# Early loads into a larger buffer class, convolution and gate tiles in turn, and the last expert tiles by token half, in a two-block transformer kernel

## The chip, the cores and the metric

The kernel runs as one program on one core of one Trainium2 chip. The metric is the time of one execution on the device in microseconds (us), of which lower is better.

## The reference, cut to what is computed

Two blocks run one after the other on a batch of one with 256 tokens (T) of width 1024 (D), all in float32. The first block is a gated mixer, whose two halves (block attention MoBA and a chunked mLSTM) read projections of one normed and modulated input; the modulation rows come from a product with `ada_w`. The second block adds a memory cross-attention and a PEER expert layer, twice, and a last norm:

```python
mod = jnp.dot(silu(c), ada_w[l]) + ada_b[l]                  # 6 rows of 1024
h = modulate(rms_norm(x, norm1_g[l]), sh1, sc1)
z = jnp.einsum('bsd,de->bse', h, w_in[l]) + b_in[l]
mq, mk, mv, mo, mi, mf, aq, ak, av, ga, gb = split(z)
qk = silu(causal_dwconv(concat([mq, mk]), conv_w[l], conv_b[l]))
ya = moba_attention(rope(aq), rope(ak), av)                  # 8 heads, softmax over 256 keys
ym = rms_norm(mlstm_chunkwise(q, k, mv, mi, mf)) * sigmoid(mo)
merged = sigmoid(ga) * (ym @ p_mlstm[l]) + sigmoid(gb) * (ya @ p_moba[l])
x = x + g1 * (merged @ w_out[l])
...                                                          # gated feed-forward, then block two
for l in range(2):
    h = h + mixer(rmsnorm(h)); h = h + memory_cross_attn(rmsnorm(h), rmsnorm(mem), wq, wkv, wo)
    h = h + peer_ffn(rmsnorm(h), wq, sub_keys, u, v)         # 128 tiles of 128 experts
return rmsnorm(h, final_norm)
```

## The kernel before, in words

**Products.** A weight tile of 128 by 1024 numbers is loaded as part of a 1 MB transfer (`raw`, two tiles each), issued on SP's queue by `stream()` (L358). `split()` makes of each tile a rounded copy `wH` on ACT (L335) and the rest `wL` on DVE (L336). TensorE (PE) then makes three products for each 128x128 piece: L400 (`nH`, `wH`), L401 (`nL`, `wH`) and L402 (`nH`, `wL`), where `nH` and `nL` are the same two parts of the input. `lin_t` gives an output tile with 24 such matmuls of 256 columns from one weight tile (8 pieces). `lin_n` (L430 to L432) gives the natural layout with 512 columns, 12 matmuls for a weight tile. The pool `wraw` has 3 `raw` buffers; `wspl` has 3 of `wH` and 3 of `wL`. Everything with pool `None` lies in size classes: the largest, `c2064`, has 12 buffers.

**First block, in order.** `mem_kv(0)` makes the keys of the memory from `wk0`, unsplit, in one pass of f32 matmuls (L398), and the values from `wv0` (`lin_n`). While the generator `kv` steps through 12 steps, the loop in `first_block` puts other work between them: `ada` steps, each of which loads 1 MB of `ada_w` and makes two rows with two DVE instructions (`adaj`, L598, 128x1024); `rope_tables` at step `RI` = 5 (some fifteen DVE instructions, then cosine and sine on ACT); and from step 4 on one `n1.chunk` a step. A chunk squares a part of x on ACT (L219) and adds it on POOL, and the eighth on DVE (L223). `n1.sums` sums over the partitions on PE (L203); `n1.bc` takes the power on POOL (L473, `pow_col`), and PE (L460) and DVE (L465) spread it as `rbc`.

Then `w_in` is multiplied. Its 37 transposed tiles come in the order in which `w_in_t` is packed: the mLSTM gates, 8 rotary tiles (RoPE), 8 convolution tiles, 4 output gates (`smo`), 16 merge gates (`sg`). `evac` takes a tile out of PSUM. A convolution tile costs ACT three instructions and DVE four (`conv`, L699 three times and L702); a gate tile costs ACT one. The natural tiles `w_in_n` are four weight pairs: two before, and two later in `rest()`, after 8 of the tiles that follow. From the ninth tile on, these products are the *filler* of `moba` (L955 scores, `sme` softmax on DVE and ACT in L483 to L491, L500 transposes, L512 to L514 values) and `mlstm`. Every third filler step adds an `ada` step (`AS` = 3); what is left of the 12 later `ada` steps runs in `w_out` (`AW` = 3).

**PEER and end.** In `v_tile`, 128 expert tiles are accumulated into four PSUM banks `y` (token half `tb` by output half `hf`), 12 matmuls of 512 columns each (L1500), first all of token half 0, then of 1. After layer 0, four copies (`py`, L1525), transposes (L1531) and adds to x (L1533) follow. After layer 1, `final` adds y to x (L1625), squares (L1627), takes the power, multiplies by r and the norm's row in one DVE instruction (L1633), and writes out.

The order on each engine is made by a scheduler from the program; each engine then runs its own list in that order.

Of the kernel before, what the change touches and what calls it, by code (L numbers as in the profile page):

```python
# [17 lines left out]
ALU = mybir.AluOpType  # L18
# [12 lines left out]
VL, RI, MD, UX, M1, M2, D1, D2, AS, AW, PQ0, NQ0, FT, F0, FH, FS, FL, FO = 6, 5, 1, 4, 1.25, 1.5, 0.5, 0.75, 3, 3, 13, 3, 0.6, 1, 0.5, 1, 4, 1.075  # L31
# [63 lines left out]
def layout(i):  # L95
# [13 lines left out]
    A["w_in_t"] = _pack_t(np.concatenate([gate, w_in[:, 2056:3080], w_in[:, 0:1024], w_in[:, 1536:2048], w_in[:, 3592:5640]], axis=1))  # L109
# [174 lines left out]
class Prog:  # L284
# [73 lines left out]
    def stream(self, name, head=None, split=True, order=None):  # L358
        ap = self.A[name]
        n = ap.shape[0]  # L360
        for i in [2 * j for j in order] if order else range(0, n, 2):
            k = min(2, n - i)
            if head is None or i:
                raw = self.t(self.wraw, "raw", [P, 2, 1024])
                self.nc.sync.dma_start(raw[:, :k], ap[i:i + k].rearrange("n p f -> p n f"))
            else:
                raw = head
# [202 lines left out]
    def mem_kv(self, l, nm, head=None):  # L570
# [12 lines left out]
        if head is None:  # L583
            yield from self.lin_t(f"wk{l}", 8, 8, nm.hs, evac, norm=nm)
        else:
            yield from self.lin_t(f"wk{l}", 8, 8, None, evac, st=self.stream(f"wk{l}", head, False), norm=nm, whole=self.memg)
# [66 lines left out]
    def first_block(self):  # L653
# [16 lines left out]
        for i in range(12):  # L670
            next(kv)
            if i % 3:
                next(ada)
            if i == 1:
                nc.sync.dma_start(self.x, A["xT"])
            if i == RI:
                cos, sin = self.rope_tables()
            if 4 <= i:
                n1.chunk(i - 4)
        n1.sums()  # L680
        n1.bc
# [32 lines left out]
        def evac(e, ps):  # L714
# [9 lines left out]
            elif e < 17:  # L724
                raw = self.t(None, "qraw", [P, T])
                nc.scalar.activation(raw, ps, AF.Identity, bias=self.vec("b_qk", e - 9))  # L726
                conv(e - 9, raw)
            elif e < 21:
                nc.scalar.activation(smo[:, e - 17], ps, AF.Tanh, scale=0.5, bias=hb[:, e - 17:e - 16])
            else:  # L730
                nc.scalar.activation(sg[:, e - 21], ps, AF.Tanh, scale=0.5, bias=hb[:, e - 17:e - 16])
# [20 lines left out]
        def rest():  # L752
            for _ in range(8):
# [34 lines left out]

        for g in (self.lin_t("p_moba", 8, 4, (ya[:, :4], ya[:, 4:]), ev_ma), self.lin_t("p_mlstm", 8, 4, (ym[:, :4], ym[:, 4:]), ev_mm)):
            self.run(g)  # L790
# [5 lines left out]
        for i, _ in enumerate(self.lin_t("w_out", 8, 8, (mH, mL), self.residual(n2, lambda e: self.mod[:, 16 + e:17 + e]))):  # L796
            if i % AW == AW - 1:
# [567 lines left out]
    def peer(self, l, nm):  # L1365
# [117 lines left out]

        def v_tile(n):
# [11 lines left out]
            for tb in range(2):  # L1496
                sl = slice(tb * P, tb * P + P)
                for a, m in ((wh, vH), (wh, vL), (wl, vH)):
                    for hf in range(2):
                        nc.tensor.matmul(y[tb * 2 + hf], a[:, sl], m[:, hf * 512:hf * 512 + 512], start=n == 0 and a is wh and m is vH, stop=n == P - 1 and a is wl)  # L1500
# [21 lines left out]
        for g in range(2):  # L1522
            for tb in range(2):
                yt = self.t(None, "py", [P, 512])
                (nc.scalar.copy if tb else nc.vector.tensor_copy)(yt, y[tb * 2 + g])  # L1525
                ys.append(yt)
        for g in range(2):
            for tb in range(2):
                ps = self.sm()
                for c in range(4):  # L1530
                    nc.tensor.transpose(ps[:, c * P:c * P + P], ys[g * 2 + tb][:, c * P:c * P + P], self.ident)  # L1531
# [86 lines left out]
    def final(self, y, xn, frow):  # L1618

        nc = self.nc  # L1620
        for tb in range(2):
            ss = self.t(None, "fss", [P, 2])
            for hf in range(2):
# [3 lines left out]
                nc.scalar.activation(junk, xs, AF.Square, accum_out=ss[:, hf:hf + 1])  # L1627
            nc.vector.tensor_add(ss[:, :1], ss[:, :1], ss[:, 1:])
            r = self.pow_col(ss[:, :1], 1.0 / D, EPS, 1)
            for hf in range(2):  # L1630
                sl = slice(hf * 512, hf * 512 + 512)
                o = self.t(None, "fo", [P, 512])
                nc.vector.scalar_tensor_tensor(out=o, in0=xn[:, tb, sl], scalar=r, in1=frow[:, sl], op0=ALU.mult, op1=ALU.mult)  # L1633
# [29 lines left out]
```

## Time and profile before

| | us |
|---|---|
| median of 3 runs (lowest to highest) | 2528.02 (2525.88 to 2528.76) |
| the profiled execution's own time | 2529.0 |
| its span in the trace | 2527.3 |
| PE busy | 2481.3 (98%) |
| DVE busy | 1887.2 (75%) |
| ACT busy | 1293.1 (51%) |
| POOL busy | 94.5 (4%) |

The span is what the trace covers; the time holds 1.7 us more. Busy times are of the engine's own instructions, and PE's contain matmuls that overlap. In the chain of waits that ended last, PE has 82% of the span and DVE 8%; in the groups by line, the expert products L1500 are the largest, and the line with most idle time of PE ahead of it is L398 (the memory's keys).

### The profile page before, as it was taken

Reading aid. Unit: us, or ns where it says so; the run is one execution under the profiler, and the core shown is the slowest. Engines: PE = TensorE matmul, PEld = TensorE weight load, DVE = VectorE, ACT = ScalarE, POOL = GpSimd, SP = SyncE. Lnnn points to the kernel's source line nnn. Section 1 sums busy time; section 2 is a strip of 40 time slices with the busy share of each in tenths; the row PEclk is TensorE's granted clock in tenths of the full one; section 3 lists DMA queues with packets and bytes.
Section 4 is the critical chain, followed back from the end, with each engine's and each line's share of the span. In section 5 each row is a group of like instructions: output and inputs, shape, how many; then the busy total and the mean of one; then the engine's idle time right before and its main releaser. Section 6 shows DMA issues by size and latency. Waiting matters only on the chain.

```text
span 2527.3 us, 44009 instructions
## 1 busy us (share of the span) xinstructions
PE 2481.3 (98%) x17668; PEld 2297.1 (91%) x17668; DVE 1887.2 (75%) x3438; ACT 1293.1 (51%) x2102; POOL 94.5 (4%) x107
## 2 busy tenths in 40 slices
PE   8999999999999999999999999999999999999998
PEld 6879999999999999999888889899999989998887
DVE  7887876686898976555777798767999755556776
ACT  3554555455455555444444563645455544444544
POOL 1000100221000000000000100110000000000000
PEclk9999999999999999999999999999999999999999
DMA  8556565554555796567875544345457866579753
GB/s 336 183 181 229 204 230 205 184 169 150 173 175 199 273 313 221 194 222 241 296 257 193 191 172 150 117 150 167 168 192 270 312 221 212 202 241 298 277 187 130
DMA packets 197468, 536.20 MB, mean 212 GB/s; under 512 B 9232, under 2 KB 82192, under 8 KB 191760
## 3 DMA queue, kind: packets, MB, share of 16 engines
q1 hardware_dynamic: 197264, 533.40, 61.2%
q8 instruction: 138, 2.26, 0.4%
q14 instruction: 66, 0.54, 0.1%
HBM read 492.47 MB, written 40.89 MB: 211 GB/s over the span
## 4 chain that ended last, share of the span: by engine, by line
PE 82%; DVE 8%; issue 6%; DMA 2%; ACT 1%; POOL 0%; SPq 0%; DVEq 0%; POOLq 0%; ACTq 0%
PE mm L1500 23%; PE mm L400 9%; PE mm L401 9%; PE mm L402 9%; PE sm L400 8%; PE sm L401 8%; PE sm L402 8%; DVE wL L336 2%; PE sm L1462 1%; PE sm L1463 1%; PE mm L431 1%; PE mm L432 1%; PE mm L430 1%; DMA gt<-gate_dram 1%; DMA raw<-in_wk 1%
## 5 line engine op out<-in xcount | busy, mean ns | idle before, releaser
L335 ACT CAST wH<-raw 128x1024 fp32r<-128x1024 f32 x789 | 826.6, 1049 | 992.4 <-PE sm L401 312.9
L336 DVE TENSOR_TENSOR wL<-raw,wH 128x1024 fp32r<-128x1024 f32 x789 | 966.8, 1226 | 455.4 <-ACT wH L335 449.8
L400 PE MATMUL sm<-uH,wH 128*128 128x256 f32 x2048 | 584.3, 285 | 2.1 <-ACT wH L335 2.0
L402 PE MATMUL sm<-uH,wL 128*128 128x256 f32 x2048 | 577.3, 282 | 3.8 <-DVE wL L336 3.8
L401 PE MATMUL sm<-uL,wH 128*128 128x256 f32 x2048 | 578.6, 283 | 0.0
L400 PE MATMUL mm<-nH,wH 128*128 128x256 f32 (+1 forms) x1432 | 410.6, 288 | 4.6 <-ACT qraw L726 2.4
L401 PE MATMUL mm<-nL,wH 128*128 128x256 f32 (+1 forms) x1432 | 404.8, 283 | 1.2 <-DVE nL L616 1.0
L402 PE MATMUL mm<-nH,wL 128*128 128x256 f32 (+1 forms) x1432 | 403.6, 283 | 0.8 <-DVE wL L336 0.6
L400 PEld LDWEIGHTS sm<-uH,wH 128*128 128x128 f32 x2048 | 386.3, 189 | 6.6 <-ACT wH L335 2.5
L402 PEld LDWEIGHTS sm<-uH,wL 128*128 128x128 f32 x2048 | 386.0, 189 | 5.6 <-DVE wL L336 5.6
L401 PEld LDWEIGHTS sm<-uL,wH 128*128 128x128 f32 x2048 | 386.7, 189 | 3.6
L1500 PE MATMUL mm<-wH,pwh 128*128 128x512 f32 x1024 | 317.6, 391 | 4.0 <-ACT pwh L335 4.0
L1500 PE MATMUL mm<-wL,pwh 128*128 128x512 f32 x1024 | 316.8, 391 | 0.0
L1500 PE MATMUL mm<-wH,pwl 128*128 128x512 f32 x1024 | 316.3, 390 | 0.0
L400 PEld LDWEIGHTS mm<-nH,wH 128*128 128x128 f32 x1432 | 270.1, 189 | 9.8 <-issue 3.5
L401 PEld LDWEIGHTS mm<-nL,wH 128*128 128x128 f32 x1432 | 270.9, 189 | 2.1 <-DVE nL L616 1.2
L402 PEld LDWEIGHTS mm<-nH,wL 128*128 128x128 f32 x1432 | 270.2, 189 | 2.5 <-DVE wL L336 1.4
L1500 PEld LDWEIGHTS mm<-wL,pwh 128*128 128x128 f32 x1024 | 192.8, 188 | 41.2
L1500 PEld LDWEIGHTS mm<-wH,pwl 128*128 128x128 f32 x1024 | 192.5, 188 | 41.0
L1500 PEld LDWEIGHTS mm<-wH,pwh 128*128 128x128 f32 x1024 | 185.8, 188 | 37.3 <-ACT pwh L335 4.4
L1493 DVE TENSOR_TENSOR pw<-act,gt 128x256 f32<-128x256 f32 x256 | 108.6, 424 | 19.9 <-DMA gt<-gate_dram 12.6
L336 DVE TENSOR_TENSOR pwl<-pw,pwh 128x256 fp32r<-128x256 f32 x256 | 108.8, 425 | 12.6 <-ACT pwh L335 6.6
(452 smaller groups left out, 3085.6 us busy)
## 6 DMA issues: line engine op xcount, KB each, us to landing
raw<-in_u SPq DMA_DIRECT2D x128, 1024.0 KB, 5.0
raw<-in_v SPq DMA_DIRECT2D x128, 1024.0 KB, 5.0
gate_dram<-gstg SPq DMA_DIRECT2D x32, 1024.0 KB, 4.8
gt<-gate_dram SPq DMA_DIRECT2D x32, 1024.0 KB, 8.3
raw<-in_ada SPq DMA_DIRECT2D x24, 1024.0 KB, 4.9
raw<-in_w_gu SPq DMA_DIRECT2D x22, 1024.0 KB, 4.9
raw<-in_w_in_t SPq DMA_DIRECT2D x18, 1024.0 KB, 5.1
raw<-in_pq SPq DMA_DIRECT2D x16, 1024.0 KB, 5.0
```

Source lines behind the costliest of these rows:

```text
L335: self.nc.scalar.copy(H, src)
L336: self.nc.vector.tensor_sub(L, src, H.bitcast(F32))
L400: mm(ps[:, :w], H[:, o:o + P], xH[:, c], start=c == 0, stop=False)
L401: mm(ps[:, :w], H[:, o:o + P], xL[:, c], start=False, stop=False)
L402: mm(ps[:, :w], L[:, o:o + P], xH[:, c], start=False, stop=c == kc - 1)
L430: mm(pss[tb], xh, H[:, o:o + 512], start=c == 0, stop=False)
L431: mm(pss[tb], xl, H[:, o:o + 512], start=False, stop=False)
L432: mm(pss[tb], xh, L[:, o:o + 512], start=False, stop=c == kc - 1)
L1462: nc.tensor.matmul(ps[:, k * P:k * P + P], at(ah), at(o1), start=True, stop=False)
L1463: nc.tensor.matmul(ps[:, k * P:k * P + P], at(al), at(o1), start=False, stop=True)
L1493: nc.vector.tensor_mul(w.rearrange("p (c t) -> p c t", c=16), act[b][:, j].rearrange("p (c t) -> p c t", c=16), box[b][:, :, j])
L1500: nc.tensor.matmul(y[tb * 2 + hf], a[:, sl], m[:, hf * 512:hf * 512 + 512], start=n == 0 and a is wh and m is vH, stop=n == P - 1 and a is wl)
```

## The change

It does five things. (1) `stream` may take its buffers from `c2064`, and `wk0` now does, so that `wraw` holds only its first tile until `wv0`. (2) In the loop of `first_block` the `ada` steps stand at other steps, `rope_tables` at step 3, the eight chunks two at a time at steps 4 to 7, and the sums and the spread row at steps 9 and 10 instead of behind the loop. (3) `w_in_t` is packed so that convolution and `sg` tiles alternate for 16 tiles; `smo` and the other `sg` follow; the second half of `w_in_n` comes after 16 tiles instead of 8. (4) Of the `ada` steps that were left, one runs in `p_moba` and one in `w_out`. (5) The products of the last 3 expert tiles are kept back and made as all of token half 0, then all of token half 1; `py` copies go by token half; `final` multiplies by the row before r is known, and then by r, half of it on ACT.

```diff
-    def stream(self, name, head=None, split=True, order=None):
+    def stream(self, name, head=None, split=True, order=None, pool=True):
+        home = self.wraw if pool else None
...
-                raw = self.t(self.wraw, "raw", [P, 2, 1024])
+                raw = self.t(home, "raw", [P, 2, 1024])
...
-            if i % 3:
+            if i in (1, 4, 5, 6, 7, 8, 9, 10):
                 next(ada)
-            if i == 1:
+            if i == 3:
+                cos, sin = self.rope_tables()
+            if i == 4:
                 nc.sync.dma_start(self.x, A["xT"])
-            if i == RI:
-                cos, sin = self.rope_tables()
-            if 4 <= i:
-                n1.chunk(i - 4)
-        n1.sums()
-        n1.bc
+            if 4 <= i < 8:
+                n1.chunk(2 * i - 8)
+                n1.chunk(2 * i - 7)
+            if i == 9:
+                n1.sums()
+            if i == 10:
+                n1.bc
...
-            elif e < 17:
+            elif e < 25 and e % 2:
+                c = (e - 9) // 2
                 raw = self.t(None, "qraw", [P, T])
-                nc.scalar.activation(raw, ps, AF.Identity, bias=self.vec("b_qk", e - 9))
-                conv(e - 9, raw)
-            elif e < 21:
+                nc.scalar.activation(raw, ps, AF.Identity, bias=self.vec("b_qk", c))
+                conv(c, raw)
+            elif 24 < e < 29:
...
         def rest():
-            for _ in range(8):
+            for _ in range(16):
                 yield next(zt)
             yield from zn
             yield from zt
...
         for g in (self.lin_t("p_moba", ...), self.lin_t("p_mlstm", ...)):
-            self.run(g)
+            for i, _ in enumerate(g):
+                if i == 3 and not moved:
+                    moved.append(next(ada, None))
...
         for i, _ in enumerate(self.lin_t("w_out", ...)):
-            if i % AW == AW - 1:
+            if i == 3:
                 next(ada, None)
...
+            rest.append([(hf, a, m, ...) for a, m in ((wh, vH), (wh, vL), (wl, vH)) for hf in range(2)])
+            if n < P - 3:
+                products(0)
+                products(1)
+                rest.clear()
+            elif n == P - 1:
+                products(0)
+                for p in rest:
+                    p.sort(key=lambda q: q[0])
+                products(1)
...
+            xf = [self.t(None, "fx", [P, 512]) for _ in range(2)]
+            for hf in range(2):
+                nc.vector.tensor_mul(xf[hf], xn[:, tb, hf * 512:hf * 512 + 512], frow[:, hf * 512:hf * 512 + 512])
             nc.vector.tensor_add(ss[:, :1], ss[:, :1], ss[:, 1:])
             r = self.pow_col(ss[:, :1], 1.0 / D, EPS, 1)
...
-                nc.vector.scalar_tensor_tensor(out=o, in0=xn[:, tb, sl], scalar=r, in1=frow[:, sl], op0=ALU.mult, op1=ALU.mult)
+                if hf:
+                    nc.vector.tensor_scalar(o, xf[hf], r, None, op0=ALU.mult)
+                else:
+                    nc.scalar.activation(o, xf[hf], AF.Copy, scale=r)
```

**The first place: PE, where the memory's values begin.** `sm_167` is the sum of x's squares, `sm_450` and `sm_432` the spread power, `mm_340` to `mm_353` the values from `wv0`. Before, third weight tile of `wv0`:

```order
L432 MATMUL mm_341<-wL_370,nH_140 128x512
L203 MATMUL sm_167<-ones,sq_256 128x1 x2
L430 MATMUL mm_340<-wH_390,nH_140 128x512
L431 MATMUL mm_340<-wH_390,nL_141 128x512
L430 MATMUL mm_341<-wH_390,nH_140 128x512
L431 MATMUL mm_341<-wH_390,nL_141 128x512
L460 MATMUL sm_450<-ident,pr_90_447 128x128 x2
L432 MATMUL mm_340<-wL_391,nH_140 128x512
```

With the change, between the last keys and the first weight tile of `wv0`:

```order
L399 MATMUL mm_306<-memg_108,raw_307 128x256 x8
L399 MATMUL mm_330<-memg_108,raw_307 128x256 x8
L203 MATMUL sm_167<-ones,sq_279 128x1 x2
L461 MATMUL sm_432<-ident,pr_82_404 128x128 x2
L431 MATMUL mm_352<-wH_356,nH_140 128x512
L432 MATMUL mm_352<-wH_356,nL_141 128x512
L431 MATMUL mm_353<-wH_356,nH_140 128x512
L432 MATMUL mm_353<-wH_356,nL_141 128x512
```

The sum and the spread stood among the products of the values, with products ahead of and behind them; now both stand ahead of the first of them. On DVE the eighth add of the squares, which waits for POOL's six, now stands ahead of four `adaj`, then `pa`, `rbc` and only then the first `wL` of `wv0`; before, that add and `pa` stood behind the first two `wL`.

**The second place: PE, at the end of the block attention.** `mm_1919` and `mm_1956` are gate tiles, `mm_1877` and `mm_1878` the first half of the natural tiles that follow. Before:

```order
L500 MATMUL sm_1949<-ident,sme_1771 128x128 x2
L512 MATMUL sm_1988<-pT_1822,vnat_580 64x128
L513 MATMUL sm_1988<-pT_1822,vnat_580 64x128
L514 MATMUL sm_1988<-pT_1822,vnat_580 64x128
L500 MATMUL sm_1995<-ident,sme_1864 128x128
L400 MATMUL mm_1956<-nH_538,wH_1959 128x256
L401 MATMUL mm_1956<-nL_539,wH_1959 128x256
L512 MATMUL sm_2070<-pT_1953,vnat_580 64x128
L513 MATMUL sm_2070<-pT_1953,vnat_580 64x128
L402 MATMUL mm_1919<-nH_538,wL_1921 128x256
```

With the change:

```order
L515 MATMUL sm_1988<-pT_1874,vnat_580 64x128
L501 MATMUL sm_1995<-ident,sme_1906 128x128
L513 MATMUL sm_2070<-pT_1967,vnat_580 64x128
L514 MATMUL sm_2070<-pT_1967,vnat_580 64x128
L515 MATMUL sm_2070<-pT_1967,vnat_580 64x128
L501 MATMUL sm_1995<-ident,sme_1916 128x128 x2
L513 MATMUL sm_2076<-pT_1999,vnat_580 64x128
L514 MATMUL sm_2076<-pT_1999,vnat_580 64x128
L915 MATMUL sm_2155<-qk_579 128x256
L916 MATMUL sm_2155<-qk_579 128x128
L431 MATMUL mm_1877<-wH_1947,nH_538 128x512
L432 MATMUL mm_1877<-wH_1947,nL_539 128x512
```

The last heads' transposes and values, which had gate products between them and 44 more of these ahead of the last head, now stand together, and a natural tile follows whose weights were loaded late.

**The third place: DVE, in `w_out`.** `nL` and `x_res` are the residual's instructions. Before:

```order
L451 SCALAR_TENSOR_TENSOR x_res<-mm_2988,mod,x_res 128x256
L598 ISA adaj_3064,mod<-raw_3060,cb_159 128x1024
L598 ISA mod 128x1
L336 TENSOR_TENSOR wL_3071<-raw_3068,wH_3070 128x1024
L237 SCALAR_TENSOR_TENSOR nL_2872<-x_res,geff_2834,nH_2871 128x256
```

With the change:

```order
L336 TENSOR_TENSOR wL_3034<-raw_2996,wH_3033 128x1024
L237 SCALAR_TENSOR_TENSOR nL_2878<-x_res,geff_2840,nH_2877 128x256
L452 SCALAR_TENSOR_TENSOR x_res<-mm_2953,mod,x_res 128x256
L336 TENSOR_TENSOR wL_3071<-raw_3068,wH_3070 128x1024
L237 SCALAR_TENSOR_TENSOR nL_2878<-x_res,geff_2840,nH_2877 128x256
```

The two `adaj` of the last `ada` step no longer stand ahead of `wL_3071`.

## Rows read from the trace of the kernel before

**Rows 1.** Busy time of each engine in stretches of the span (from and to in us, length, then us and instructions of PE, its weight loads, DVE, ACT, POOL; the granted clock of PE; the DMA engines' share and GB/s).

```profile
0.00:50.00 50.00, 38.35 (x150) 30.97 (x150) 35.83 (x83) 16.84 (x33) 8.80 (x16) 0.93 0.93 353
50.00:100.00 50.00, 48.03 (x314) 43.56 (x313) 40.47 (x69) 25.14 (x37) 3.48 (x3) 1.00 0.55 199
100.00:150.00 50.00, 45.69 (x288) 38.85 (x286) 42.94 (x115) 29.21 (x52) 0.00 (x0) 0.97 0.55 190
300.00:350.00 50.00, 50.00 (x417) 50.00 (x417) 38.13 (x61) 28.00 (x53) 1.05 (x4) 1.00 0.62 218
```

**Rows 2.** What PE waited for over the whole span (PSUM kind and line, who released it; us in total, times, longest).

```profile
PE mm L398 <- DVE memg L556: 6.1, 1, 6.1
PE mm L400 <- ACT qraw L726: 2.4, 1, 2.4
PE mm L430 <- ACT wH L335: 2.0, 1, 2.0
PE sm L500 <- DVE sme L491: 1.0, 1, 1.0
```

**Rows 3.** Instructions in order of time from 15 to 62 us, of several engines (start, length, engine, line, what it does, how many in a row; in brackets the idle time ahead and what ended it).

```profile
15.97 0.71 POOL L473 TENSOR_TENSOR pr<-pa,mhalf 128x2 f32<-128x2 f32 x1 [14.00 <-DVE pa L471]
...
18.86 0.42 ACT L219 ACTIVATE sq<-x_res 128x256 f32<-128x256 f32 x1 [2.43 <-DMA x_res<-in_xT]
26.65 15.74 PE L398 MATMUL mm<-memg,raw 128*128 128x256 f32 x64 [2.57 <-DMA raw<-in_wk]
29.37 1.23 DVE L598 CUSTOM_DVE_ANT_0 adaj<-raw,cb 128x1024 bf16<-128x1024 f32 x1 [2.54 <-DMA raw<-in_ada]
35.51 0.37 SPq L365 DMA_DIRECT2D raw<-in_wv  x1
42.87 7.48 POOL L223 TENSOR_TENSOR sq<-sq,sq 128x256 f32<-128x256 f32 x6 [26.18 <-ACT sq L219]
44.39 0.50 PE L430 MATMUL mm<-wH,nH 128*128 128x512 f32 x1 [2.00 <-ACT wH L335]
46.45 1.22 PE L432 MATMUL mm<-wL,nH 128*128 128x512 f32 x2 [0.51 <-DVE wL L336]
47.99 1.75 DVE L598 CUSTOM_DVE_ANT_0 adaj<-raw,cb 128x1024 bf16<-128x1024 f32 x1
52.84 1.64 POOL L473 TENSOR_TENSOR pr<-pa,mhalf 128x2 f32<-128x2 f32 x1 [2.50 <-DVE pa L471]
54.54 0.43 PE L460 MATMUL sm<-ident,pr 128*128 128x128 f32 x2 [0.93 <-POOL pr L473]
61.27 3.50 DVE L336 TENSOR_TENSOR wL<-raw,wH 128x1024 fp32r<-128x1024 f32 x3 [2.47 <-ACT wH L335]
```

**Rows 4.** Busy time as in Rows 1, of the stretch in which convolution tiles and block attention run, and of eight microseconds in it.

```profile
111.70:195.00 83.30, 77.59 (x489) 63.98 (x489) 74.47 (x201) 46.49 (x103) 4.98 (x8) 0.96 0.48 173
146.00:154.00 8.00, 7.85 (x20) 5.01 (x20) 5.12 (x14) 4.11 (x10) 1.32 (x2) 0.59 0.22 92
```

**Rows 5.** Groups of DVE instructions by line in the same stretch, 111.7 to 195 us (count; busy us, mean ns of one; idle us ahead of them and what ended it).

```profile
L336 DVE TENSOR_TENSOR wL<-raw,wH 128x1024 fp32r<-128x1024 f32 x18 | 21.9, 1214 | 0.8 <-ACT wH L335 0.7
L598 DVE CUSTOM_DVE_ANT_0 adaj<-raw,cb 128x1024 bf16<-128x1024 f32 x12 | 14.8, 1243 | 0.0
L702 DVE SCALAR_TENSOR_TENSOR qk<-ra,qk 128x256 f32<-128x256 f32 x8 | 3.6, 452 | 2.4 <-ACT ra L701 2.4
```

**Rows 6.** Instructions in order of time in that stretch, PE and DVE (columns as in Rows 3).

```profile
141.59 0.39 PE L400 MATMUL mm<-nH,wH 128*128 128x256 f32 x1 [2.38 <-ACT qraw L726]
...
151.17 0.55 DVE L892 TENSOR_SCALAR wt<-sm,ucol 128x256 f32<-128x256 f32 x1 [2.55 <-PE sm L890]
```

**Rows 7.** Instructions in order of time in `w_out`, 280 to 291 us, POOL, DVE and PE (columns as in Rows 3).

```profile
280.08 0.75 POOL L223 TENSOR_TENSOR sq<-sq,sq 128x256 f32<-128x256 f32 x1 [35.75 <-ACT sq L219]
...
287.85 1.21 DVE L598 CUSTOM_DVE_ANT_0 adaj<-raw,cb 128x1024 bf16<-128x1024 f32 x1
...
288.99 1.73 DVE L336 TENSOR_TENSOR wL<-raw,wH 128x1024 fp32r<-128x1024 f32 x1
290.78 0.38 PE L402 MATMUL mm<-mH,wL 128*128 128x256 f32 x1 [1.64 <-DVE wL L336]
```

**Rows 8.** Instructions in order of time behind the last expert tile of layer 0, DVE and PE (columns as in Rows 3).

```profile
1432.60 1.28 DVE L1525 COPY py<-mm 128x512 f32<-128x512 f32 x2
...
1433.34 1.96 PE L1531 MATMUL sm<-ident,py 128*128 128x128 f32 x16 [0.29 <-DVE py L1525]
```

**Rows 9.** Instructions in order of time at the end, 2517 to 2527 us, PE, DVE, POOL and SP's queue (columns as in Rows 3).

```profile
2517.75 0.61 PE L1500 MATMUL mm<-wH,pwl 128*128 128x512 f32 x2
2518.25 1.28 DVE L1625 TENSOR_TENSOR xn<-xn,mm 128x512 f32<-128x512 f32 x2 [0.16 <-ACT fj L1627]
2519.60 0.61 ACT L1627 ACTIVATE fj<-xn 128x512 f32<-128x512 f32 x1
...
2520.45 1.42 DVE L1633 SCALAR_TENSOR_TENSOR fo<-xn,pr,frow 128x512 f32<-128x512 f32 x2 [0.66 <-POOL pr L473]
2521.24 3.34 SPq L1634 DMA_DIRECT2D out<-fo  x4
...
2522.21 0.56 POOL L473 TENSOR_TENSOR pr<-pa,mhalf 128x1 f32<-128x1 f32 x1 [1.79 <-DVE pa L471]
2522.80 1.41 DVE L1633 SCALAR_TENSOR_TENSOR fo<-xn,pr,frow 128x512 f32<-128x512 f32 x2 [0.67 <-POOL pr L473]
```

## What the change should do to the time, and why

> **What bounds the kernel.** I read first the stretches of 50 us [rows 1]. From 300 us on PE is busy in every microsecond, 417 matmuls of 256 columns in 50.00 us, one each 0.12 us; nothing that this change touches can gain there. PE has holes before: 11.7 us in the first 50, 2.0 in the next, 4.3 from 100 to 150. So the first 300 us and the two ends of the expert layers are all that is for sale. Second, the list of what PE waited for [rows 2]: the longest entry, 6.1 us for the memory's first columns, is not touched. The others are small: what can be won is some ten or twenty us at the very most, 0.4 to 0.8% of the time. Third, the rows in order of time at those places [rows 3, 6, 7], to see which engine was late.
>
> Up to 70 us, DMA and DVE set the pace. Transfers leave one behind the other: x has landed at 18.86 and the fourth megabyte behind it releases DVE at 29.37 [rows 3], 2.6 us per MB. From 111.7 to 195 us the pace is DVE's: it is busy 74.5 of 83.3 us [rows 4]. That part of PE's list asks for 314 matmuls of 256 columns (37.7 us), 48 of 512 at twice that (11.0) and some 62 small ones (about 12.5): 61.2 us. PE is shown busy for 77.6, since its clock was low in part (0.59 granted from 146 to 154, between the levels of 1.2 and 2.4 GHz [rows 4]) and its matmuls overlap. I read this so: PE cannot end the stretch before DVE has split the last weight, and DVE needs 74.5 plus its own idle 8.8.
>
> **1. Scratch buffers, rotary tables, norm: 0 to 72 us.** The rotary tables stood on DVE behind four `ada` steps and now stand behind one. Three steps of two `adaj`, 1.2 us each [rows 5], and the wait of 2.54 [rows 3] go from ahead of them: 9.7 us. POOL's first add comes at about 33 instead of 42.87 [rows 3]. Six adds took 7.48 us [rows 3], so the sum is ready near 40. Then come four `adaj` (4.6 us), two key evacuations (0.8), the power (0.71 alone, 1.64 beside DVE [rows 3]), the spread row, and the first `wL`: its product starts near 48.4, against 46.45 [rows 3]. **+2.0**. PE has the keys done earlier, near 39, as the last transfer of `wk0` comes one place earlier in the queue; but PE's list is in order, and the power's transpose now stands ahead of the values. So the early keys buy nothing. What comes back: the power no longer interrupts the values (0.93 idle at 54.54 [rows 3]), and DVE, which idled 2.47 us at 61.27 [rows 3], has its modulation ready before the first `w_in_t` tile, where PE waited about 1 us for `nL`. **-2.0**. Against this, four `adaj` now stand between the second and the third weight of `wv0`, 4.6 us where PE has 5.5 us of work: **+0.5**. Sum **+0.5**. Bounds: with adds at 0.75 each, as one alone takes [rows 7], the first product isn't late and -2.5 is left; with all at the slow rate, +5 (rival 2). The transfer of `wv0` that was issued at 35.51 [rows 3], since its buffer came free late, leaves earlier; it lands before it is needed in both, so I cost it at nothing.
>
> **2. Convolution and gate tiles in turn: 100 to 235 us.** A 256-column tile takes PE 24 times 0.12 = 2.9 us. A convolution tile asks DVE for a `wL` of 1.2 and four instructions near 0.47 [rows 5], 3.1 us, ahead of all softmax and `ada` work; a gate tile asks 1.2. Eight convolution tiles in a row therefore put DVE behind, and each later tile pays the debt back. The debt at its largest sets what PE loses. Before, it is largest at the third gate tile, the end of the stretch in [rows 4]: DVE 74.5 + 8.8 idle against PE 61.2, so 22.1 us, less the lead that DVE had at its start (the same in both). After the change I counted the rows of both lists from the same weight on. The debt is largest at the first late natural tile: there DVE has two `wL`, two `adaj` [rows 5], thirteen small softmax pieces and two natural evacuations less to do, 8.4 us, and PE has 44 products of 256 columns more (+5.3), 44 of 512 fewer (-10.1) and fewer small ones (-2.2): 7.0 us less. The debt without idle falls by only 8.4 - 7.0 = **1.4 us**, since the same work is on DVE and only moves against PE's. The rest depends on the 8.8 us that DVE idled. Of these, 2.4 are waits for the tanh of a convolution [rows 5], which a gate tile between gives time for, and 2.55 came behind PE at the low clock [rows 6]. Nearest are these rows: I take 2.8 as gone. Sum **-4.2**; bounds -10.2 (all idle gone) and +2 (none gone, and the waits of rival 1).
>
> **3. `ada` steps out of `w_out`.** Two `adaj` stood ahead of the `wL` that PE waited 1.64 us for [rows 7]; they are gone there: -1.6. The step that goes into `p_moba` puts 2.4 us on DVE ahead of a weight, and its megabyte ahead of that weight's own on SP's queue; between 0 (the `wL` is early) and 1.2 comes back, and I take 0.4. **-1.2**, bounds -2.0 and 0.
>
> **4. End of the first expert layer.** The last three tiles' weights stay in all three buffer pairs until the end, so the next layer's first `wL` comes among the `py` copies and the transposes' start (idle 0.29 now [rows 8]) or their adds move by part of a 1.2 us `wL`. The copies on two engines (1.28 for two on DVE [rows 8]) give some back. **+0.3**, bounds -0.5 and +1.
>
> **5. The end.** PE's last matmul stays at 2518.36. Before, DVE multiplied token half 0 for 1.42 us from 2520.45 while half 1 had its squares done at 2520.2, and the power of half 1 came at 2522.21 [rows 9]. Now half 0 is ready during the 18 matmuls of half 1 (4.1 us). Half 1: last add to 2519.0, squares to 2519.9, two `fx` products on DVE to 2520.3, sum and power (0.35 + 0.6) to 2521.3, both output halves side by side to 2522.1 instead of 2524.21. Two issues on SP's queue behind each other (four took 3.34 [rows 9]) keep 0.6 to 0.8 of that. **-1.3**, bounds -2.0 and -0.3.
>
> **Sum.** +0.5 - 4.2 - 1.2 + 0.3 - 1.3 = -5.9. The profiled execution's own time is 2529.0, so 2523.1; the median of the runs is 1.0 below that execution, so **2522.1**.
>
> **Rivals.**
>
> *1. The waits only move (no change).* For it: the scheduler puts the last heads' transposes and values side by side, with no gate product between, and a natural tile behind them whose transfer is issued behind an `ada` step. Each turn PE, ACT, PE costs about the 1.0 us that PE waited for `sme` [rows 2], twice; the natural weight perhaps 2.4, like the wait at 141.59 [rows 6]. Against it: DVE is late there anyway, so part of these waits lies under the debt. If no idle of DVE goes: part 2 becomes +2, the sum +0.3, time **2528.3**. Chance 0.25.
>
> *2. POOL's chain holds PE (slower).* The place is the eighth add on DVE, which blocks DVE until POOL is through. It decides if that add comes later than about 42 us. Beside `adaj`, which then takes 1.75 instead of 1.2, POOL's instructions take 1.64 [rows 3]; six of them from 33 on end at 42.8, four slow `adaj` and the power bring the first product to 52, +5.5; 2.0 comes back as above, and a longer idle time of PE costs about 2 more at the low clock, as it did at 26.65 and 44.39: after each of these waits [rows 3] the clock fell (0.93 granted in the first 50 us [rows 1]). So part 1 is +5, and with part 2 at +2 the sum is +4.8 to +5.5: **2533**. Against it: the six adds took 7.48, not 9.8, and DVE, once it stands at that add, disturbs no more. Chance 0.11.
>
> The Trainium skill ("SBUF — State Buffer", Who interferes with whom) speaks against the change here: a DVE instruction with two inputs in SBUF and a POOL instruction that reads SBUF exclude each other, and the loser stands still for the whole of the other. By it each of the six adds could wait out an `adaj`, 6 times (0.75 + 1.2) = 11.7 us, an estimate that would make this rival about 2535. The trace agrees that they hinder each other, but shows both longer, 1.75 and 1.64, and six adds in 7.48.
>
> *3. DVE's idle time goes wholly.* Alternation was worth most where DVE waited for ACT. Part 2 near -9, part 1 near -2.5: sum -13.7, **2514.3**. Chance 0.17.
>
> **Chances.** My own case, 2519 to 2525, has 0.47. About 0.2%, 5 us, is what a measurement of this kernel can tell from no change, so faster means below 2523.0 and slower above 2533.1. Faster: 0.34 of my case's 0.47 and all of rival 3: 0.51. Same: 0.13 of my case, 0.22 of rival 1 and 0.02 of rival 2: 0.37. Slower: 0.09 of rival 2 and 0.03 of rival 1: 0.12. The range goes from rival 3 to just past rival 1, **2514 to 2530**; some 0.05 lies below and 0.13 above.
>
> **What would show it.** In the changed trace: POOL's six adds starting near 33; the first L431 of the values near 47 and its L433 near 48; the `w_in_t` tiles starting within 1 us of before, 72; from there to 235 us, PE's holes smaller by about 4 us and DVE's idle below 7; no wait of PE above 0.7 in `w_out`; the last matmul to the end 7.6 us instead of 8.9. It is wrong if PE waits at the spread power past 49 us, if the L501 and L513 rows near 200 us carry waits of 1 us and more, or if PE's holes after 300 us change.

## The result, and the profile after

The changed kernel takes **2513.03 us** (median of 5 runs, 2511.72 to 2516.41), the kernel before 2528.02: a ratio of 0.9942, 95% interval 0.993 to 0.9953. It is faster by 15.0 us where the forecast had 5.9, and the time is 1 us below the range. The profiled execution takes 2513.03 us, its span is 2511.3.

Stretches of the changed kernel (columns as in [rows 1]; these lines answer to [rows 1, 4]):

```profile
0.00:50.00 50.00, 36.79 (x155) 30.58 (x156) 35.73 (x86) 16.22 (x33) 10.34 (x18) 0.97 0.96 368
50.00:100.00 50.00, 48.17 (x314) 43.59 (x313) 39.02 (x66) 26.31 (x38) 0.00 (x0) 1.00 0.53 185
100.00:150.00 50.00, 49.66 (x332) 43.17 (x330) 44.45 (x124) 31.98 (x61) 1.04 (x1) 1.00 0.53 189
300.00:350.00 50.00, 50.00 (x415) 50.00 (x414) 40.57 (x67) 27.93 (x56) 0.56 (x5) 1.00 0.62 221
111.70:195.00 83.30, 80.59 (x547) 68.57 (x548) 77.26 (x206) 48.99 (x108) 8.87 (x8) 1.00 0.54 188
```

From 111.7 to 195 us PE now issues 547 matmuls instead of 489 (some of these are shorter ones that came later before; in columns the stretch holds 8.5% more), and DVE idles 6.0 us instead of 8.8. The granted clock is 1.00 where it was 0.96, since the stretch at 0.59 is gone: from 146 to 154 us it is 1.00. That is what term 2 asked for. From 300 to 350 us nothing is gained, as foretold.

What PE waited for over the whole span of the changed kernel (answers to [rows 2]):

```profile
PE mm L399 <- DVE memg L557: 6.1, 1, 6.1
PE sm L403 <- DVE wL L336: 6.1, 9, 1.6
PE mm L1521 <- ACT pwh L335: 5.0, 2, 2.8
PE sm L461 <- POOL pr L474: 4.6, 2, 3.6
PE mm L399 <- DMA raw<-in_wk: 3.5, 2, 1.7
```

The memory's first columns wait as before, and the wait for `qraw` is gone. The wait for the power (L461) has grown from at most 1.0 to 3.6. The next view shows it in order of time (answers to [rows 3]):

```profile
24.81 7.14 PE L399 MATMUL mm<-memg,raw 128*128 128x256 f32 x32 [1.74 <-DMA raw<-in_wk]
...
31.68 6.48 POOL L223 TENSOR_TENSOR sq<-sq,sq 128x256 f32<-128x256 f32 x6 [16.11 <-ACT sq L219]
32.58 1.70 DVE L599 CUSTOM_DVE_ANT_0 adaj<-raw,cb 128x1024 bf16<-128x1024 f32 x1
...
44.00 0.72 POOL L474 TENSOR_TENSOR pr<-pa,mhalf 128x2 f32<-128x2 f32 x1 [5.85 <-DVE pa L472]
...
44.77 0.69 PE L461 MATMUL sm<-ident,pr 128*128 128x128 f32 x2 [3.60 <-POOL pr L474]
...
47.11 1.09 PE L433 MATMUL mm<-wL,nH 128*128 128x512 f32 x2
```

POOL's six adds take 6.48 us from 31.68, and L433 comes at 47.11 (forecast: 7.48 from 33, and 48.4). The order is as foretold: the power stands ahead of the values, and PE pays 3.60 for it. The first `w_in_t` product comes 0.65 us later than before (71.14 against 70.49).

The end (answers to [rows 9]):

```profile
2503.36 0.73 ACT L1660 ACTIVATE fo<-fx,pr 128x512 f32<-128x512 f32 x1 [1.35 <-POOL pr L474]
...
2503.76 1.28 DVE L1646 TENSOR_TENSOR xn<-xn,mm 128x512 f32<-128x512 f32 x2
2503.87 4.62 SPq L1661 DMA_DIRECT2D out<-fo  x4
...
2506.58 0.55 POOL L474 TENSOR_TENSOR pr<-pa,mhalf 128x1 f32<-128x1 f32 x1 [3.25 <-DVE pa L472]
2507.17 0.72 ACT L1660 ACTIVATE fo<-fx,pr 128x512 f32<-128x512 f32 x1 [1.36 <-POOL pr L474]
```

Half 0 is written out while half 1 still multiplies. From the last matmul to the end it is 7.1 us (8.9 before).

**Where the rest came from.** Setting the starts of PE's stages of the two traces side by side, the changed kernel is ahead by 6.9 us at the first product of `ya`, 7.1 at the first expert keys, 10.1 at the end of layer 0 and 14.2 at the last matmul. So some 7 us are gained in the two expert layers, where PE has few waits and its instructions stand in the same order but for the last three tiles. There the matmuls themselves became shorter. The page's groups of the expert keys' products, both layers (us busy, mean ns of one, idle ahead), before and after:

```profile
L400 PE MATMUL sm<-uH,wH 128*128 128x256 f32 x2048 | 584.3, 285 | 2.1 <-ACT wH L335 2.0
L402 PE MATMUL sm<-uH,wL 128*128 128x256 f32 x2048 | 577.3, 282 | 3.8 <-DVE wL L336 3.8
L401 PE MATMUL sm<-uL,wH 128*128 128x256 f32 x2048 | 578.6, 283 | 0.0
```

```profile
L401 PE MATMUL sm<-uH,wH 128*128 128x256 f32 x2048 | 579.9, 283 | 2.1 <-ACT wH L335 2.0
L403 PE MATMUL sm<-uH,wL 128*128 128x256 f32 x2048 | 574.0, 280 | 6.1 <-DVE wL L336 6.1
L402 PE MATMUL sm<-uL,wH 128*128 128x256 f32 x2048 | 574.9, 281 | 0.0
```

Idle time ahead of them even grew; each takes 2 ns less. Matmuls overlap, so what they cost PE's list is the step from the start of one to the start of the next. Added up over a layer's 3072 products, this **key sum** is 377.2 and 374.7 us before (layers 0 and 1), and 372.8 and 371.2 after. Six or seven steps of a layer are longer than 0.3 us, most of them waits for a weight. Without these the sums are 370.9 and 367.9 before, 364.6 and 362.7 after: the other steps gave 11.5 us, of which longer waits took 3.6 back. What differs for these products is where `uH` and `uL` lie: part 1 takes three more buffers from `c2064`, so everything later is dealt other buffers. In the built programs, per partition, `uH`/`uL` begin at bytes 126720/134976 and 101952/93696 before, and at 110208/93696 and 168000/101952 after.

### The profile page after: what moved, and what is told of

Same layout as the page of the kernel before. It is cut to its first block, busy times and chain, and to the rows that moved or that the text cites. A ratio compares the mean times of both kernels' runs of the same rounds, so it can differ in the third digit from the quotient of the medians.

```text
span 2511.3 us, 44014 instructions
## 1 busy us (share of the span) xinstructions
PE 2466.0 (98%) x17668; PEld 2285.8 (91%) x17668; DVE 1884.0 (75%) x3440; ACT 1294.4 (52%) x2104; POOL 96.5 (4%) x107
## 4 chain that ended last, share of the span: by engine, by line
PE 82%; DVE 8%; issue 6%; DMA 3%; ACT 1%; POOL 0%; SPq 0%; POOLq 0%; DVEq 0%; ACTq 0%
PE mm L1521 23%; PE mm L401 9%; PE mm L402 8%; PE mm L403 8%; PE sm L401 8%; PE sm L403 8%; PE sm L402 8%; DVE wL L336 2%; DMA raw<-in_ada 1%; PE sm L1471 1%; PE sm L1472 1%; PE mm L433 1%; PE mm L431 1%; PE mm L432 1%; DMA gt<-gate_dram 1%
## 5 line engine op out<-in xcount | busy, mean ns | idle before, releaser
L335 ACT CAST pwh<-pw 128x256 fp32r<-128x256 f32 x256 | 102.4, 400 | 31.5 <-DVE pw L1504 31.5
```

What stands on the lines that cost most here:

```text
L335: self.nc.scalar.copy(H, src)
```

## The experiments

Parts are numbered here as in the change, terms as in the prediction. Unless it says otherwise, a ratio stands against runs of the kernel before on the same chip; its 95% interval is in brackets. The experiments ran on several chips (the kernel before had medians of 2527.58 to 2528.39 there), so a difference of two changed kernels' medians is good to some us only.

Theory P (placement): the byte offset of the operands in SBUF sets the step, and part 1 gains by moving buffers. Rival L (local): the gain is made by what the parts do in their own stages.

### One part at a time

*tiles_only*: the kernel before with part 3 alone (`w_in_t` packed in turn, `evac`, `rest`).

```diff
-            elif e < 17:
+            elif e < 25 and e % 2:
...
-            for _ in range(8):
+            for _ in range(16):
```

> The kernel before with the third part alone (convolution and gate tiles in turn, the natural tiles after 16). uH and uL lie where they lay. Theory: from the block attention's first scores to p_moba 6.2 us are gained, as in the changed kernel, the products uH/uL stay at 377 and 375, time 2521 to 2522.5. Rival (alternation gains only together with the earlier norm and the moved ada steps): 2 to 3 us gained, 2525 to 2526. Rival execution: the gain up to 300 us is 6, but the end is anywhere from 2515 to 2523.

2525.08 us, ratio 0.9988 (0.9979 to 0.9997): 2.9 us gained, less than the 6 expected and inside the rival's 2525 to 2526. In the one trace it is 4.7 us ahead at the first product of `ya` (the block attention's output).

*no_tiles*: the changed kernel with these lines as before.

> The changed kernel without its third part (w_in_t packed as before, eight convolution tiles in a row). uH and uL lie where they lie in the changed kernel. Theory: 6 us come back between the first scores and p_moba, time 2518 to 2520, the expert products as in the changed kernel (372.8 and 371.2). Rival (the norm and ada steps gave it): 2514 to 2516.

2518.49 us, 0.9958 (0.9945 to 0.9972): 5.5 above the changed kernel. Key sums 372.6 and 371.0, nearly as there. So part 3 is worth some 3 to 5 us.

*no_scratch*: the changed kernel without part 1.

```diff
-            ... st=self.stream(f"wk{l}", head, False, pool=False) ...
+            ... st=self.stream(f"wk{l}", head, False) ...
```

> The changed kernel without its first part: wk0's transfers stay in the three wraw buffers; uH and uL lie at the offsets of before. Theory placement: the expert products stand at 377 and 375 as before, which costs 8 us; the first 72 us lose 0 to 3 (wv0's transfers wait for buffers again); time 2520 to 2524. Rival execution: only the first 72 us lose, 2513 to 2516.

2525.84 us, 0.999 (0.9981 to 0.9999): **12.8 us are lost**, more than by any other part tried alone and more than expected, though its own stage shows only 1.5 us at the first `w_in_t` product and 2.8 at the first expert keys. The offsets are those of the kernel before again, and so are the key sums: 378.3 and 374.6.

*end_only*: the kernel before with part 5 alone (kept-back tiles, copies, `final`).

```diff
+            if n < P - 3:
+                products(0)
+                products(1)
+                rest.clear()
```

> The kernel before with the fifth part alone (last three expert tiles by token half, final norm in two steps on two engines). uH and uL lie where they lay. Theory: from the last matmul to the end of the span 7.1 us instead of 8.9, as in the changed kernel; behind layer 0's last expert tile no change within 0.5; time 2526 to 2526.8. Rival (the shorter end came from something else in the changed kernel): 2528.

2528.31 us, 1.0 (0.9991 to 1.0009). The stretch behind the last matmul is 1.8 us shorter (7.12 for 8.92), but the time doesn't show it: single runs of the kernel before scatter from 2523.2 to 2532.6.

### Other buffers and nothing else

One memset of one column for each of N buffers, used for nothing, deals all later tiles other buffers.

```diff
+        for _ in range(N):
+            nc.gpsimd.memset(self.t(None, "spare", [P, 8, T])[:, 0, :1], 0.0)
         self.cb = self.t(None, "cb", [P, D])
```

*turn5*: the kernel before, N = 5, which puts layer 0's `uH` and `uL` where the changed kernel has them.

> The kernel before, plus five one-column memsets by POOL, each on a fresh c2064 buffer at the very start, so that the class is dealt out in another turn: in layer 0 the expert input uH, uL then lies at the offsets that it has in the changed kernel. Theory placement: the products uH/uL of layer 0 (377.2 us before by the distances between their starts, 372.8 in the changed kernel) come to about 373, and the time falls by 3 to 5 us, to 2523 to 2525. Rival execution (the step varies from run to run whatever lies where): 2528 within 1.5, products at 377 or by chance elsewhere. Rival waits (all of the gain stems from waits in the changed stages): 2528.

2518.45 us, 0.996 (0.9947 to 0.9974): **9.9 us faster than its own runs of before (2528.31) with no part of the change in it**, and by the interval 6.6 to 13.4. That is more than the 3 to 5 expected. Key sums 372.1 and 372.9, 6.9 us lower in all; layer 1, which moved to a third place, gained too.

*spare_no_scratch*: no_scratch with N = 5.

> The changed kernel without its first part (no_scratch, 2525.84 us), with five one-column memsets at the start that each take one buffer of the large class and are used for nothing, so that layer 0's uH and uL lie at the changed kernel's bytes 110208 and 93696 and layer 1's at 143232 and 118464 (turn5's). If part 1 is worth its 12.8 us only because it moves the class on (placement): the products of the expert keys take 372 to 373 us in layer 0 and 372 to 374 in layer 1 in place of 378.3 and 374.6, and the time is 2514 to 2519. If part 1 gains by what it does in the first 72 us and in front of p_moba: 2524 to 2528 as no_scratch, with the products at 377 to 378.

2515.9 us, 0.9959 (0.9945 to 0.9973): by the medians 9.9 of part 1's 12.8 us are back (7.8 of 12.1 by the ratios), key sums 371.2 and 374.0. P holds for most of what part 1 gains; L can be right for the rest alone. The same stretch of layer 0, 700 to 900 us, of no_scratch and of spare_no_scratch (columns as in [rows 1]):

```profile
700.00:900.00 200.00, 197.35 (x1841) 194.99 (x1840) 185.43 (x374) 114.67 (x182) 0.00 (x0) 1.00 0.64 226
```

```profile
700.00:900.00 200.00, 196.84 (x1861) 194.45 (x1861) 185.19 (x369) 115.56 (x183) 0.00 (x0) 1.00 0.67 233
```

The clock is 1.00 in both and PE is shown busy for 197 of 200 us in both, yet it issues 20 matmuls more in the second.

*spare6_after* and *spare8_after*: the changed kernel, N = 6 and 8.

> The changed kernel with six such memsets at the start: layer 0's uH and uL at bytes 126720 and 143232, layer 1's at 168000 (as in the changed kernel) and 134976. Nothing that the change does is taken back. If place decides, the key products' sums move from 372.8 and 371.2 us by up to 6 in a layer (126720 is where uH lay in the kernel before, with 377.2), and the time by the same, to 2513 to 2522. If the gain beyond the changed stages is something else that the change does: 2513 to 2516 with the sums as they were.

2514.39 us, 0.9948 (0.9935 to 0.9962); key sums 374.8 and 370.9. Layer 0 moved by 2, less than the 6 allowed; layer 1, where only `uL` moved, by nothing.

> The changed kernel with eight such memsets: layer 0's uH stays at 110208 and layer 1's at 168000, uL goes to 126720 and 118464. If uH's place alone decides, sums and time stay (372.8, 371.2; 2512 to 2516); if uL's place, or how the two stand to each other, counts, the sums move by 1 us or more in a layer and the time with them (2510 to 2522).

2513.89 us, 0.9947 (0.9933 to 0.996); key sums 372.1 and 372.1. Nothing that the times could tell, and these two alone would leave the rule open.

### Which property of the place

Three paddings looked for it. The large class gets 2080 columns (so that its buffers are a multiple of 128 bytes apart), for which the class of 256 columns gives one buffer; a pad tile may shift what follows.

```diff
-    CLASSES = (... (256, 14), ... (2064, 12))
+    CLASSES = (... (256, 13), ... (2080, 12))
...
+        nc.gpsimd.memset(self.mem.tile([P, 16], F32, tag="shift", name="shift", bufs=1), 0.0)
```

*pad0_before* (no shift tile):

> The kernel before with the largest buffer class widened from 2064 to 2080 columns (8320 bytes, a multiple of 128, instead of 8256), and one buffer fewer in the 1 KB class to make room; no other edit, the buffers are dealt out in the same turn. All twelve then begin at a multiple of 128 bytes, where before every second one begins 64 bytes off. Theory remainder: the products go at the shorter step when uH and uL begin at the same remainder by 128 bytes; both layers come from 377 and 375 us to 371 to 373, time 2518 to 2521. Rival neighbours (buffers side by side, or which buffers are read, decide): they lie side by side as before, so 377 and 375 stay, 2527 to 2529.

2522.99 us, 0.9985 (0.9976 to 0.9994); key sums 371.0 and 375.0. Layer 0 gained 6 us, layer 1 nothing, though in both layers `uH` and `uL` now have the same remainder by 128: that form of the theory falls.

*pad64_before* and *pad64_after* (all classes shifted by 64 bytes):

> As pad0_before, and all scratch shifted by 64 bytes, so that all twelve large buffers begin 64 bytes past a multiple of 128 and the weight copies wH, wL (another pool) at a multiple of 128, as in layer 1 of the changed kernel, where the median step was the same for all eight pieces. Theory remainder: both layers 371, time 2517 to 2520, not above pad0_before. Rival neighbours: 377 and 375, 2527 to 2529.

> The changed kernel with the same widened class and shift: all pairs of large buffers at the same remainder, not only uH and uL. Theory remainder: other products whose two inputs lay at unequal remainders (nH and nL of the mixers and the cross-attention) gain too, uH/uL stay near 371 to 372; time 2509 to 2513. Rival: only uH/uL mattered, 2512 to 2514.

2539.92 us, 1.0043 (1.0029 to 1.0057), and 2529.16, 1.0 (0.9991 to 1.0009): both far slower than expected. Key sums are low (372.4 and 372.2; 373.1 and 368.2), but the expert values' products, with `pwh` and `pwl` as the stationary operand (the one that PE's weight loads read; the other is the moving one), went from a median step of 227 ns to 233: 3072 times 6 is 18 us. I took the remainder of 64 by 128 of `pwh` for the cause.

*keys64*: the changed kernel with the classes of pad0_before and a shift of 64 for the large class alone, taken back behind it.

```diff
+        if first:
+            nc.gpsimd.memset(self.mem.tile([P, 16], F32, tag="back", name="back", bufs=1), 0.0)
```

> The changed kernel with all twelve buffers of the large class begun 64 bytes past a multiple of 128, and every other class at a multiple of 128 (pad64_after had those at 64 too, and lost at the expert values' products, whose pwh and pwl lie in a small class). If bytes alone decide: the key products as in pad64_after (373.1 and 368.2 us for the layers against 372.8 and 371.2 in the changed kernel), the value products back at 227 ns each instead of 233, the time 2506 to 2513, faster than the changed kernel. If pad64_after's loss was not pwh's and pwl's bytes but the size of the class (2080 columns for 2064): 2525 to 2530 as pad64_after.

2526.1 us, 0.9997 (0.9988 to 1.0006): **a miss**. `pwh` lay at a multiple of 128, and its products were as slow as in the pad64 kernels. Sorting the key sums of all these kernels by the offsets' remainder by **256** put them in order, and `pwh` too: 128 in the quick kernels, 192 in the pad64 ones, 0 here. Three of the next four kernels tested that; swap tests the place alone.

*swap*: no_scratch, N = 7, which exchanges the two layers' places.

> no_scratch (2525.84 us) with seven one-column memsets at the start, which exchange the layers' places: layer 0's uH and uL at 101952 and 93696 (the kernel before's layer 1; remainders by 256: 64 and 0), layer 1's at 126720 and 134976 (its layer 0; 0 and 64). If place decides: the sums of the key products change over from 378.3 and 374.6 to 374 to 375 and 377 to 379, and the time stays at 2523 to 2528. If the layers differ for another reason: the sums stay.

2523.26 us, 0.9982 (0.9973 to 0.9991); key sums 374.7 and 376.8: they changed over with the bytes.

*keys128*: keys64 with a second pad of 48 columns for 16.

> keys64 (2526.1 us) with the other classes begun 128 bytes later and nothing else changed: pwh and pwl leave a remainder of 128 by 256, as in the changed kernel, where keys64 had 0 and pad64_after 192; uH and uL stay at remainders 192/192 in layer 0 and 64/64 in layer 1. If the remainder by 256 decides: the value products back from 396 ns busy (some 233 ns a step) to 391 (227), the key products as in keys64 (373.0 and 368.8 us), time 2507 to 2515. If the large class at 64 bytes past a multiple of 128 is what slows the value products: 2523 to 2530 as keys64.

2517.03 us, 0.9957 (0.9943 to 0.997), 9.1 below keys64 and 2 above what was expected; the value products are back at 227 ns. Layer 1's key sum is 372.6, not the 368.8 expected: 3.8 of the 6 us by which the time lies above the middle of what was expected.

*pwh64*: the changed kernel with a 64-byte pad behind the large class's first buffer.

> The changed kernel with a 64-byte pad behind the first buffer of the large class: the large class stays where it was, all other classes begin 64 bytes later, so pwh and pwl leave 192 by 256 in place of 128. If their remainder decides: key products as in the changed kernel (372.8 and 371.2 us), value products at some 233 ns a step in place of 227, 3072 of them, so 2513 + 18: 2525 to 2533. If the large class was to blame in pad64_before, pad64_after and keys64: 2511 to 2517.

2527.87 us, 1.0001 (0.9992 to 1.001): 14.8 us lost by moving the small classes 64 bytes. The key sums are 372.7 and 367.9; layer 1's was expected to stay at 371.2. One group of value products of the changed kernel, of pwh64 and of keys128 (us busy, mean ns):

```profile
L1521 PE MATMUL mm<-wH,pwl 128*128 128x512 f32 x1024 | 318.0, 391 | 0.0
```

```profile
L1523 PE MATMUL mm<-wH,pwl 128*128 128x512 f32 x1024 | 323.7, 396 | 0.0
```

```profile
L1524 PE MATMUL mm<-wH,pwl 128*128 128x512 f32 x1024 | 317.5, 390 | 0.0
```

*keys256*: the changed kernel, every large buffer at remainder 64, the small classes at 128.

```diff
+    CLASSES = ((32, 14), (128, 7), (256, 12), (512, 8), (1024, 4), (2112, 12))
...
+        ... self.mem.tile([P, 48], F32, tag="shift", ...)
+        ... self.mem.tile([P, 16], F32, tag="back", ...)
```

> The changed kernel with the large class's buffers at 2112 columns (8448 bytes, a multiple of 256), shifted so that each leaves 64 by 256 in both layers, and the small classes as in the changed kernel (128); for the room two buffers of 256 columns and one of 128 fewer. If the remainder decides: both layers' key products as layer 1 in keys64 (368 to 369.5 us each), 2513 less 6.4: 2503 to 2511. If the low sum belonged to layer 1 and not to its bytes: layer 0 at 371 to 373, time 2508 to 2514. If the classes with fewer buffers make engines wait: above 2514.

**2500.08 us, 0.9894 (0.9879 to 0.9909)**: 13 us below the changed kernel and the best of all, better than expected. Yet the key sums are 370.8 and 372.6, hardly lower, where 368 to 369.5 was expected: the time was met by another road. Most of the gain is in the other operands that lie in large buffers, as `nH` and `nL`; the groups of the changed kernel and of keys256:

```profile
L401 PE MATMUL mm<-nH,wH 128*128 128x256 f32 x1080 | 310.0, 287 | 2.5 <-ACT nH L236 1.6 <-ACT wH L335 0.8
L402 PE MATMUL mm<-nL,wH 128*128 128x256 f32 x1080 | 305.3, 283 | 0.1
```

```profile
L401 PE MATMUL mm<-nH,wH 128*128 128x256 f32 x1080 | 308.0, 286 | 2.5 <-ACT nH L236 1.6 <-ACT wH L335 0.8
L402 PE MATMUL mm<-nL,wH 128*128 128x256 f32 x1080 | 303.0, 281 | 0.1
```

In steps, the mean over the products with `nH` or `nL` (4296, those with a step above 300 ns left out) falls from 121.9 to 119.8 ns, 9 us in all.

So the rule by 256 foretold the value products in both kernels that were made for them (keys128, pwh64). For the key products with `uH` and `uL` both at 64 its forecast failed three times, in keys128, pwh64 and keys256.

## Why the prediction was wrong

**The step that failed** is the sentence on the stretch from 300 us on: "nothing that this change touches can gain there". It counted what PE waits for and took a matmul's own length (one each 0.12 us) as given. Part 1 was priced by what it does in the first 72 us (+0.5); that it deals all later tiles other buffers was not priced at all. The price is measured twice without the rest of the change: turn5 gained 9.9 us on the kernel before (interval 6.6 to 13.4), and spare_no_scratch 9.9 on no_scratch. The pair of traces agrees: the changed kernel's key sums are 7.9 us lower, and its value products, whose mean step fell from 227.6 to 226.8 ns, 2.5. Without 9.9, 15.0 - 9.9 = **5.1 us are left for the parts, against a sum of 5.9**. That is an estimate, good to some 4 or 5 us by the two intervals, and turn5 has layer 1 at another place than the changed kernel. So the one term that was missing is the larger part of the miss, and nothing shows another that was far off.

The sentence was also wider than its row, which ends at 350 us. The kernel before does wait later, in its expert layers:

```profile
PE mm L1500 <- ACT pwh L335: 4.0, 2, 2.7
PE sm L402 <- DVE wL L336: 3.8, 8, 1.0
```

These waits grew with the change (5.0 and 6.1 above), so the gain isn't there; but the sign that the prediction named, holes after 300 us that change, did come.

- *Term 1, +0.5* (parts 1 and 2): +0.65 at the first `w_in_t` product. The order of events is the one given (early adds, the power ahead of the values), but the sum is right partly by luck: L433 comes only 0.66 later (47.11 for 46.45) where +2.0 was forecast, and of the -2.0 and +0.5 that were to follow nothing shows.
- *Term 2, -4.2* (part 3): from the first score to the first product of `ya` the changed kernel gains 6.2 us. Of this not all is the turn. Six kernels with eight convolutions in a row show +0.1 to -3.1 there against the kernel before, on average -1.9 (end_only, the kernel before up to there, shows -2.7), and the twelve with the turn -2.7 to -8.2, on average -5.5; the difference is **-3.7**. The size is right, and no_tiles and tiles_only (5.5 and 2.9) lie about it. The debt of 22.1 us is too large: the trace has 338 products of 256 columns, 51 of 512 and 100 smaller ones in [rows 4]'s 489, and the prediction counted 314, 48 and 62. The term goes by differences and doesn't use it. Rival 1's waits did come, 0.63 and 0.46 at L513, but the stretch gained all the same.
- *Term 3, -1.2* (part 4): `w_out` has one wait of 0.32 left (1.64 in [rows 7]), worth 2.0; `p_moba` pays 1.0 for the step that it got. -1.0.
- *Term 4, +0.3* (the layer's end): from the end of the last value product of layer 0 to the first product of the next layer it is 3.45 us instead of 3.16, +0.3.
- *Term 5, -1.3* (the end): -1.8 in the trace. SP's four issues now take 4.62 us, but start early enough (2503.87).
- *Rival 2*: POOL's adds took 6.48, not 9.8, and the power came in time. Only two of the six began beside an `adaj` (1.70 and 1.40 long instead of 1.22); these two took 1.59 and 1.58, the other four 0.72 or 0.73. The Trainium skill ("SBUF — State Buffer", Who interferes with whom) states that such instructions exclude each other, and the trace agrees for these two. The prediction's 11.7, an estimate, took an `adaj` beside each add.
- *Rival 3* gave 2514.3, near the time, but by luck: its reason isn't the one, as DVE still idles 6.0 us.

## What to carry to other kernels

A stretch in which an engine hardly waits is not closed to a change. Whatever takes one buffer more from a shared class can move every later operand, and here that alone was worth 9.9 us, about two thirds of the gain. So before crediting an edit, give its placement to the kernel without it (a few unused buffers do). And set the placement by hand, since the best one found, keys256, gained 13 us on the changed kernel with no instruction moved on purpose.

## What the runs showed that I had not expected

In these kernels a matmul's step goes with the remainder by 256 of the byte offset of its operands. The stationary `wH`, `wL` of the key products leave a remainder of 128 in every kernel here. The key sums by the remainders of `uH` and `uL`, 18 kernels with two layers each; the third column leaves out the five to nine steps of a layer above 0.3 us:

| `uH` / `uL` | key sum, us | without steps above 0.3 us | layers |
|---|---|---|---|
| 0 / 64 | 376.8 to 378.3 | 370.4 to 371.9 | 5 |
| 0 / 128 | 374.8 to 375.0 | 369.4 to 369.6 | 2 |
| 64 / 0 | 374.2 to 374.7 | 367.9 | 5 |
| 128 / 192 | 372.9 to 374.0 | 367.1 | 2 |
| 192 / 192 | 372.3 to 373.1 | 365.0 to 365.1 | 3 |
| 64 / 192 or 192 / 64 | 372.1 to 372.4 | 365.0 | 3 |
| 128 / 0 | 371.0 to 372.8 | 364.4 to 364.8 | 7 |
| 64 / 64, `pwh` at 128 | 370.8 to 372.6 | 361.0 to 364.1 | 6 |
| 64 / 64, `pwh` at 0 or 192 | 367.9 to 368.8 | 358.3 to 359.6 | 3 |

In five of the nine lines the spread all but vanishes in the third column: it was waits. Seven layers at 128 / 0, at three pairs of places and on at least four chips, agree within 0.4 us, and 0 / 128 lies 5 us above 128 / 0, so the remainder by 128 is not enough. The table was drawn up after the runs; what it foretold and missed is said above.

For the value products (moving `wH`, `wL` at 128) the mean step is 226.7 to 228.0 ns with `pwh` and `pwl` at 128 (14 kernels) and 232.0 to 233.3 with 0 or 192 (4 kernels).

Two things stay open. The runs show that the place decides (turn5, swap and pwh64 change nothing else but a few memsets), and that the remainder by 256 puts the results in order; what inside the chip makes it so, none of them shows. And the last two lines of the table differ by some 3 to 4 us with the same `uH` and `uL`: in the changed kernel and pwh64 they even lie at the same bytes, with 362.7 and 358.3 us. The place of `pwh`, or of something else in the small classes, reaches into the key products of layer 1, and I did not find out how.
